# A streaming encoder layer on one core: two more block pairs by Strassen products, sums of activations started a step sooner, and a planner that counts GpSimd

## The chip, the cores and the metric

The kernel runs on one core of a Trainium2 chip. The metric is the time of the device in microseconds (us) for one execution, as the median of three runs. Everything is float32 in the inputs and outputs.

## The reference

One layer with 1024 channels on 640 rows (512 of a prompt, 8 sequences of 16 rows), with a LayerNorm ahead of it. One wide projection of the rows, `w_in` of 1024 x 6656, feeds three branches and three gates:

```python
z = x @ w_in
xa, ya, glu, q, gates = jnp.split(z, COL_SPLITS, axis=-1)
xa_c = causal_depthwise_conv(concat([conv_a_prev, xa]), conv_a_w, conv_a_b)        # width 4
h, h_last = rg_lru(xa_c, h_prev, ...)                 # gates by block matmuls, then a scan over positions
out_a = (h * jax.nn.gelu(ya)) @ proj_a
u = glu[..., :D_CONV] * jax.nn.sigmoid(glu[..., D_CONV:])
v = causal_depthwise_conv(concat([conv_b_prev, u]), conv_b_w, conv_b_b)            # width 31
out_b = jax.nn.silu(layer_norm(v, ln_b_g, ln_b_b)) @ proj_b
out_c = mem_cross_attention(q, k, v) @ proj_c         # 4 heads, 256 memory rows
g = jax.nn.sigmoid(gates + b_gate)
merged = g[:, :, 0] * out_a + g[:, :, 1] * out_b + g[:, :, 2] * out_c
x = layer_norm(ALPHA * x + merged @ w_out)
x = layer_norm(ALPHA * x + swiglu(x))
```

The outputs are the rows and the new states and memory keys and values.

## The kernel before

**Numbers and tiles.** Every matmul operand is split into a high and a low part of the type fp32r (ScalarE copies the high part, VectorE subtracts for the low part), and a product is made of three matmuls: high by high, high by low, low by high. Activations lie with channels on the partitions: `xh` and `xl` are eight blocks of 128 channels by 640 rows. A result block of 128 channels by 640 rows takes 8 channel blocks x 3 x 2 halves of 320 rows = 48 matmuls of 128x320 (a direct step, `z_step`). Weights come in through `wr` and are split to `wh` and `wl`.

**Strassen pairs.** The gate blocks of branch A are made two at a time: `Pair` holds a weight tile of 1024 x 256, and `seven` makes seven products (m1 to m7) of 12 matmuls with sums of weight quarters (`sums_1`, `sums_2`, four VectorE operations of 128x512) and sums of activation quarters. VectorE adds the results (128x320 each); `put` writes a quarter of the two result blocks, with ScalarE applying the function. The activation sums are made once, by `sums_stream`. In the first pair the products come in another order, and `m3` in a bank of its own.

**The order of the work.** The program is a list of steps (`steps`): each has a weight load, a split, matmuls and an evacuation. Between the parts of a step, `advance` lets streams emit instructions: generators for the branch work, in the order of the list `streams`. Each stream goes on while the planned time of VectorE or ScalarE, kept by the `Engine` class from fixed prices, lies behind TensorE's planned time. `yield None` ends a stream's turn until the next call. So the order on each engine is set when the program is written out, and each engine works its own queue in that order. The steps in order: branch A's inputs, query and GLU blocks, gates of branch C, `proj_c`, gates of branch B with `proj_b`, eight GELU blocks (`C_YA`, `ya_evac`), four gate pairs of branch A (`C_G`), `proj_a`, `w_out`, and the feed-forward part, which also uses pairs.

**Around the change.** `ln_b_stream` normalises branch B over its 512 channels, which lie on partitions: GpSimd adds the four channel blocks (`total`, seen at lines 853 and 855 of the profile), a matmul with `ones` sums over the partitions into a bank `pv`, and VectorE subtracts the mean; ScalarE squares, GpSimd adds again, and so on. `lru_stream` runs the convolution of width 4 (taps with `pa` on VectorE), the gates and the scan of branch A; at its end `hout` is transposed on TensorE. `a_stream` multiplies h by the GELU block and splits it (`aT`), one channel block after the other, for `proj_a`. The softmax of the attention (`nm`, exponentials, `rc`) runs beside these. Banks: `pu` is the name of four banks, two for each direct step, that are released when the step's result was evacuated; `pv` is the name of two double banks for side work, counted by `side`, `room` and `over`.

## Time and profile before

| | us |
|---|---|
| Median of three runs (their range) | 1100.15 (1099.13 to 1100.48) |
| The profiled execution's own time | 1099.67 |
| Its span in the trace | 1097.9 |
| TensorE busy | 1061.7 (97%) |
| VectorE busy | 802.9 (73%) |
| ScalarE busy | 490.1 (45%) |
| GpSimd busy | 165.3 (15%) |
| First GELU block's matmuls start | 433.5 |
| First gate pair of branch A | 490.6 |
| `proj_a` starts | 542.77 |

How to read the rows: in the engine shares, busy time, share of the span, and number of instructions. In a window: its start and end, then for PE (TensorE), PEld (weight loads), DVE (VectorE), ACT (ScalarE) and POOL (GpSimd) the busy time and the instructions, the clock that TensorE was granted, the share of busy DMA engines and their GB/s. In a timeline: start, length, engine, line, operation with output and inputs (buffer numbers left out), shapes, how many in a row, and in square brackets the idle time just before and what ended it. In a chain: start, length, engine, output. In a group: line, engine, operation and shapes with a count, busy time and mean ns of one, idle time before and what ended it. Nearly every operation of TensorE, VectorE and ScalarE is recorded at line 64, that of the helper that passes it on, so tiles and shapes tell them apart.

### The profile page before, as it was taken

What the parts mean: (1) busy time and instruction counts of PE and PEld (TensorE: products, weight loads), DVE (VectorE), ACT (ScalarE), POOL (GpSimd) and SP (SyncE); (2) the same over time, 40 slices, a digit from 0 to 9 for tenths busy, and PEclk for the clock granted to TensorE, in tenths of its full rate; (3) what the DMA queues carried; (4) which work ended last, traced back from release to release, by engine and by line L of the source; (5) the groups of instructions that cost most, each with busy time, mean ns of one, the idle gap of its engine ahead of it and who ended that gap; (6) DMA issues with size and microseconds to landing.
All of it is one profiled execution on the core that took longest, in us unless ns stands there. A gap on an engine that the chain in (4) does not pass through costs nothing.

```text
span 1097.9 us, 17000 instructions
## 1 busy us (share of the span) xinstructions
PE 1061.7 (97%) x6827; PEld 1005.9 (92%) x6827; DVE 802.9 (73%) x1335; ACT 490.1 (45%) x863; POOL 165.3 (15%) x185
## 2 busy tenths in 40 slices
PE   8799898998999999999999999899999999999997
PEld 6699898997999999999999889899999999888886
DVE  6929898996364873779855678888887887544775
ACT  4532645446648445846523124433444444334341
POOL 3623323556200000010001120000000000100111
PEclk9999999998999999999999999999999999999999
DMA  9732123352412121212325331132222322734481
GB/s 340 253 95 78 39 67 97 118 154 65 147 52 83 59 96 59 95 45 78 115 78 172 135 134 59 39 101 92 77 78 85 108 77 78 287 115 137 162 289 45
DMA packets 80334, 123.11 MB, mean 112 GB/s; under 512 B 4075, under 2 KB 59371, under 8 KB 80256
## 3 DMA queue, kind: packets, MB, share of 16 engines
q1 hardware_dynamic: 73168, 100.36, 27.6%
q0 software_dynamic: 7088, 21.68, 6.2%
q8 instruction: 53, 0.87, 0.3%
q14 instruction: 25, 0.20, 0.1%
HBM read 112.41 MB, written 9.61 MB: 111 GB/s over the span
## 4 chain that ended last, share of the span: by engine, by line
PE 70%; DVE 11%; ACT 4%; issue 1%; DVEq 0%; ACTq 0%
PE pu L64 62%; DVE s L64 10%; PE pv L64 8%; ACT s L64 3%; ACT L64 1%; DVE wl L64 1%; ACT wh L64 0%; DVE xres L64 0%; DVE mx L64 0%; DVE wh L64 0%; DVE xl L64 0%; DVE nm L64 0%; DVEq L1955 0%; ACT wl L64 0%; DVE st L64 0%
## 5 line engine op out<-in xcount | busy, mean ns | idle before, releaser
L64 PE MATMUL pu<-xh,wh 128*128 128x320 f32 x1040 | 252.6, 315 | 8.3 <-ACT s L64 7.1
L64 PE MATMUL pu<-xh,wl 128*128 128x320 f32 x1040 | 246.9, 310 | 0.0
L64 ACT ACTIVATE wh<-wr 128x1024 fp32r<-128x1024 f32 (+1 forms) x149 | 134.9, 908 | 229.1 <-PE pu L64 123.2
L64 PE MATMUL pu<-xl,wh 128*128 128x320 f32 x888 | 219.7, 311 | 0.0
L64 PEld LDWEIGHTS pu<-xh,wh 128*128 128x128 f32 x1040 | 178.1, 190 | 13.2 <-ACT s L64 9.1
L64 PE MATMUL pu<-s,wh 128*128 128x320 f32 x1064 | 185.5, 310 | 1.9 <-DVE s L64 1.3
L64 PEld LDWEIGHTS pu<-xh,wl 128*128 128x128 f32 x1040 | 177.4, 189 | 0.1
L64 DVE TENSOR_TENSOR s<-s,s 128x640 fp32r<-128x640 f32 (+4 forms) x176 | 124.5, 723 | 65.5 <-ACT s L64 63.3
L64 PEld LDWEIGHTS pu<-s,wh 128*128 128x128 f32 x1064 | 163.4, 188 | 3.4 <-DVE s L64 2.4
L64 DVE TENSOR_TENSOR wl<-wr,wh 128x1024 fp32r<-128x1024 f32 (+1 forms) x100 | 114.1, 1141 | 66.7 <-ACT wh L64 66.7
L64 PEld LDWEIGHTS pu<-xl,wh 128*128 128x128 f32 x888 | 154.2, 189 | 0.6 <-DVE xl L64 0.6
L64 DVE TENSOR_TENSOR s<-s,pu 128x320 f32<-128x320 f32 x188 | 88.4, 484 | 85.8 <-PE pu L64 83.3
L64 PE MATMUL pu<-s,wl 128*128 128x320 f32 x808 | 147.3, 310 | 0.9 <-DVE s L64 0.9
L64 DVE SCALAR_TENSOR_TENSOR s<-s,pb,s 128x511 f32<-128x511 f32 (+14 forms) x240 | 130.1, 613 | 7.8 <-ACT s L64 7.8
L64 ACT ACTIVATE s<-s 128x640 fp32r<-128x640 f32 (+4 forms) x144 | 87.9, 629 | 101.9 <-DVE s L64 101.8
L64 PEld LDWEIGHTS pu<-s,wl 128*128 128x128 f32 x808 | 126.1, 188 | 1.1 <-issue 1.1
L64 PE MATMUL pu<-wh,s 128*128 128x512 f32 (+1 forms) x396 | 116.2, 386 | 0.3 <-ACT wh L64 0.3
L64 PEld LDWEIGHTS pu<-wh,s 128*128 128x128 f32 x396 | 73.1, 189 | 15.1 <-ACT wh L64 1.2
L64 ACT ACTIVATE s<-pu 128x320 f32<-128x320 f32 (+2 forms) x90 | 36.7, 442 | 68.1 <-PE pu L64 68.0
L64 PE MATMUL pu<-wl,s 128*128 128x512 f32 (+1 forms) x198 | 62.9, 389 | 1.6 <-POOL wl L305 0.8
L305 POOL TENSOR_TENSOR wl<-wr,wh 128x1024 fp32r<-128x1024 f32 x13 | 44.4, 3418 | 81.2 <-ACT wh L64 68.4
L64 PE MATMUL pv<-wh,s 128*128 128x512 f32 (+1 forms) x152 | 48.7, 367 | 0.4 <-DVE xres L64 0.4
(139 smaller groups left out, 1249.0 us busy)
## 6 DMA issues: line engine op xcount, KB each, us to landing
wr<-in_w_in SPq DMA_DIRECT2D x26, 1024.0 KB, 5.1
wr<-in_w_ffn_down SPq DMA_DIRECT2D x19, 1024.0 KB, 5.1
wr<-in_w_ffn_gate SPq DMA_DIRECT2D x11, 1024.0 KB, 5.3
wr<-in_w_ffn_up SPq DMA_DIRECT2D x11, 1024.0 KB, 5.3
s<-in_cache_mem_k POOLq DMA_DIRECT2D x16, 256.0 KB, 7.0
s<-in_cache_mem_v POOLq DMA_DIRECT2D x16, 256.0 KB, 7.2
wr<-in_proj_a SPq DMA_DIRECT2D x4, 1024.0 KB
wr<-in_w_out SPq DMA_DIRECT2D x4, 1024.0 KB, 5.7
```

Of the source, the lines that this page charges most:

```text
L64: return f(*a, **k)
L305: self.eng.tensor_tensor(l, x, f32(h), op=OP.subtract)
```

## The change

Four edits. The GELU blocks 4 to 7 are made as two pairs, set ahead of the four gate pairs in the same call; 0 to 3 stay direct. The stream of the activation sums is put into the list one step sooner, and at its front. In the first pair of a call, which is now a GELU pair, the product m2 gets a bank of its own of the kind `pv`, and VectorE adds the copy of m1 to it. GpSimd gets an `Engine` with prices and thus a planned time; `settle(G)` makes a stream give up its turns until TensorE's planned time reaches GpSimd's, in place of one or two turns. A function `settle` with its default is new. As `G` is passed on by the helper now, its operations are recorded at line 64.

```diff
+def price_pool(e, name, a, k):
+    if name == "dma_start":
+        return 600
+    return 150 + 3.2 * elements(a[0])
...
-    G, S = nc.gpsimd, nc.sync
+    G, S = Engine(nc.gpsimd, price_pool), nc.sync
...
     def advance(few=False):
-        for e in (V, A):
+        for e in (V, A, G):
             e.time = max(e.time, state["since"])
...
+    def settle(*engines):
+
+        t = max(e.time for e in engines or (V, A))
+        yield None
+        while P.time < t:
+            yield None
...
         def total(x):
             y = get([128, T])
+            G.time = max(G.time, V.time, A.time)
             G.tensor_tensor(y, x[0], x[1], op=OP.add)
...
         y = total(vb)
         yield 1
-        yield None
+        yield from settle(G)
         yield from room()
...
         y = total(sq)
         free(*sq)
         yield 1
-        yield None
-        yield None
+        yield from settle(G)
         yield from room()
...
         G.tensor_tensor(rs, ve, mhalf[:, :5], op=OP.pow)
         yield 1
+        yield from settle(G)
         yield from room()
...
             elif n == "m2":
-                put(0, 0, p, None, None)
+                if first:
+                    put(0, 0, p, tmp["a"][:, 0], OP.add)
+                    over()
+                else:
+                    put(0, 0, p, None, None)
...
             products = [PRODUCTS[i] for i in (0, 5, 2, 1, 4, 3)] + [("m3", "x", True, "s4", "22")]
+            products[2] = ("m2", "v", True, "12", "21")
...
-                if opens:
+                if u == "v":
+                    until(lambda: side[0] < 2)
+                    acc[u] = pv()[:, 0, :HT]
+                elif opens:
                     acc[u] = pu(1)[0][:, :HT]
...
-    z_load(C_YA, 4)
-    for j in range(KD):
+    z_load(C_YA, 2)
+    for j in range(4):
         z_step(C_YA + 128 * j, ya_evac(j))
     first["pairs"] = len(steps)
-    pair_steps([(Pair(w_load(w_in, C_G + 128 * j, 7)),
+    parts_of_gel = {}
+    pair_steps([(Pair(w_load(w_in, C_YA + 128 * j, 7)),
+                 through(AF.Gelu_apprx_tanh, lambda i, j=j: slot_of(parts_of_gel, j + i),
+                         lambda i, row, j=j: gel.__setitem__(j + i, row))) for j in (4, 6)] +
+               [(Pair(w_load(w_in, C_G + 128 * j, 7)),
                  through(AF.Sigmoid, ...
...
-        if i == first["pairs"] - 6:
-            streams.insert(len(streams) - 1, ("sums0", sums_stream(lambda: state["i"] >= first["pairs"])))
+        if i == first["pairs"] - 7:
+            streams.insert(0, ("sums0", sums_stream(lambda: state["i"] >= first["pairs"])))
```

The order of the instructions changes with it. TensorE at the norm's first total (the matmul with `ones`), before; `pu<-xh,wh` and so on are matmuls of direct steps, `s_162` is GpSimd's sum, and what a row waits for stands in square brackets:

```order
L64 MATMUL pv<-s_162_2714,ones 128x512 [waits PE_49,Pool_49]
L64 MATMUL pv<-s_162_2714,ones 128x128
L64 MATMUL pu<-xh,wh 128x320 x2
L64 MATMUL pu<-xl,wh 128x320 x2
L64 MATMUL pu<-xh,wl 128x320 x2
...
L64 MATMUL pu<-xh,wh 128x320 [waits Activation_49] x2
L64 MATMUL pu<-xl,wh 128x320 x2
```

The same place now:

```order
L64 MATMUL pu<-xh,wh 128x320 [waits Activation_49] x2
L64 MATMUL pu<-xl,wh 128x320 x2
L64 MATMUL pu<-xh,wl 128x320 [waits Pool_49]
...
L64 MATMUL pv<-s_162_2714,ones 128x512 [waits PE_49,Pool_49]
L64 MATMUL pv<-s_162_2714,ones 128x128
L64 MATMUL pu<-xh,wh 128x320 x2
```

The matmul with `ones` stood 24 matmuls ahead of a step whose first matmul waits for ScalarE to release a bank; now it stands 24 behind that matmul, 48 later in all.

ScalarE at the same place, from the second table load behind the softmax's exponentials to its copies of the transposed probabilities (`pv` 128x16x16), now; `s_169` is the Sigmoid of a gate step that empties its banks, `s_183` to `s_185` are squares of the norm:

```order
L64 ACT_TABLE_LOAD
L64 ACTIVATE s_169_2766<-pu,pa 128x320
...
L64 ACTIVATE s_176_2844<-s_91_1712,pa 128x640
L64 ACTIVATE s_178_2864<-s_113_1886,pa 128x640
L64 ACTIVATE s_183_2903<-s_61_870 128x640
L64 ACTIVATE s_184_2907<-s_76_1316 128x640
L64 ACTIVATE s_185_2911<-s_116_1940 128x640
L64 ACTIVATE wh<-wr 128x1024
L64 ACTIVATE s_186_2930<-s_176_2844 128x640
L64 ACTIVATE s_179_2884<-pv 128x16x16
```

The table load and the Sigmoid stand where they stood. The squares stood ahead of the convolution's begin (`s_176`) before and now stand behind it; a copy of a convolution's result (`s_186`) came ahead of the softmax's copies. On VectorE the six taps of that convolution now stand ahead of the subtractions of the mean on which the squares wait.

VectorE at the start of `proj_a`, before; `s_347<-...,pu` adds the products of the last gate pair, `s_263_4533` is h of channel block 7, multiplied by its GELU block, and the row with `s_346` makes its low part:

```order
L64 TENSOR_TENSOR s_263_4533<-s_263_4533,s_303_5194 128x640
L64 TENSOR_TENSOR s_341_5658<-s_340_5657,pu 128x320
L64 TENSOR_TENSOR wl<-wr,wl 128x512
L64 TENSOR_TENSOR s_346_5716<-s_263_4533,s_345_5715 128x640
L64 TENSOR_TENSOR s_347_5739<-s_341_5658,pu 128x320
L64 TENSOR_TENSOR wl<-wr,wh 128x1024
L64 TENSOR_TENSOR s_344_5696<-s_341_5658,pu 128x320
L64 TENSOR_TENSOR wl<-wr,wh 128x1024
L64 TENSOR_TENSOR s_347_5739<-s_340_5657,pu 128x320
```

Now (`s_351<-s_342` is the add of the last product, `s_249` to `s_262` are h of blocks 4 to 7):

```order
L64 TENSOR_TENSOR s_351_5754<-s_342_5645,pu 128x320
L64 TENSOR_TENSOR s_350_5752<-s_226_3542,s_349_5751 128x640
L64 TENSOR_TENSOR s_249_4121<-s_249_4121,s_308_4987 128x640
L64 TENSOR_TENSOR s_353_5790<-s_249_4121,s_352_5789 128x640
L64 TENSOR_TENSOR s_254_4255<-s_254_4255,s_309_5045 128x640
L64 TENSOR_TENSOR s_355_5795<-s_254_4255,s_354_5794 128x640
L64 TENSOR_TENSOR s_259_4342<-s_259_4342,s_316_5125 128x640
L64 TENSOR_TENSOR s_357_5800<-s_259_4342,s_356_5799 128x640
L64 TENSOR_TENSOR s_262_4417<-s_262_4417,s_317_5163 128x640
L64 TENSOR_TENSOR s_359_5805<-s_262_4417,s_358_5804 128x640
```

The multiplications and low parts of blocks 4 to 7, which stood ahead of the last pair's adds, stand behind the last of them. On TensorE the transposes of `hout` move from ahead of the four gate pairs to 28 matmuls before the first of `proj_a`.

## The prediction

> **What bounds the kernel now.** I read the busy shares first, then the two stages that the change rewrites, then the place of the norm of branch B, row by row.
>
> ```profile
> PE 1061.7 (97%) x6827; PEld 1005.9 (92%) x6827; DVE 802.9 (73%) x1335; ACT 490.1 (45%) x863; POOL 165.3 (15%) x185
> ...
> 433.50:490.60 57.10, 57.06 (x389) 56.72 (x390) 43.29 (x62) 36.69 (x59) 3.69 (x8) 1.00 0.24 76
> 490.60:541.00 50.40, 48.92 (x329) 48.04 (x328) 48.47 (x80) 32.89 (x60) 0.43 (x1) 1.00 0.22 69
> ...
> 406.08 10.56 PE pu L64 x72
> ```
>
> TensorE is busy for 97% of the span, so time falls when matmuls go or when a wait of TensorE goes. In the two windows (eight GELU blocks, then four gate pairs; the columns are PE, PEld, DVE, ACT, POOL, granted clock, DMA share, GB/s) TensorE is full at full clock. VectorE has 57.10 - 43.29 = 13.8 us free in the first and 1.9 us in the second: little, if work is to be added there. A matmul of 128x320 in an unbroken run takes 10.56/72 = 0.147 us.
>
> The largest hole that the change touches is at the norm's first total:
>
> ```profile
> 253.17 2.50 PE L64 MATMUL pv<-s,ones 128*128 128x512 f32 x4 [5.00 <-POOL s L855]
> ...
> 252.61 0.54 DVE nm L64
> 253.21 1.28 ACT L64
> 254.50 1.93 ACT s L64 x8
> 256.45 1.28 ACT L64
> 257.75 0.95 ACT L64 ACTIVATE s<-pu,pa 128x320 f32<-128x320 f32 x2
> 258.58 1.70 ACT L64 ACTIVATE s<-s,rc 128x256 f32<-128x256 f32 x4
> ...
> 250.60:254.00 3.40, 0.83 (x1) 0.50 (x2) 3.37 (x5) 0.79 (x1) 2.42 (x3) 0.50 0.00 0
> 254.00:257.40 3.40, 3.40 (x12) 2.69 (x11) 1.20 (x5) 3.37 (x10) 3.40 (x5) 0.50 0.83 235
> 257.40:260.80 3.40, 3.40 (x25) 3.40 (x24) 0.83 (x3) 3.39 (x8) 2.06 (x5) 1.00 0.76 230
> ...
> 267.99 4.06 PE pu L64 x24
> 272.05 1.01 PE pv L64 x32
> ```
>
> TensorE stands from 253.17 - 5.00 = 248.17 to 253.17 for GpSimd's sum. Then the clock is at half: 0.83 us and 3.40 us of busy time at 0.50 are worth half of that, so 2.1 us more. In all 7.1 us. Meanwhile ScalarE does a table load, the exponentials of a softmax and a second table load, and only then the Sigmoid that empties a gate step's banks (257.75).
>
> **The change, part by part.** *Matmuls.* Two blocks cost 96 matmuls directly and 84 as a pair; two pairs save 24: 24 x 0.147 = **-3.5 us**, as long as TensorE sets the pace in that stage.
>
> *VectorE work of the pairs.* Prices:
>
> ```profile
> L64 DVE TENSOR_TENSOR wl<-wr,wh 128x1024 fp32r<-128x1024 f32 x8 | 9.8, 1220 | 8.6 <-ACT wh L64 8.6
> L64 DVE TENSOR_TENSOR s<-s,wr 128x512 f32<-128x512 f32 x8 | 5.5, 688 | 0.1
> L64 DVE TENSOR_TENSOR wh<-s,wh 128x512 fp32r<-128x512 f32 x8 | 5.5, 686 | 0.6 <-ACT wh L64 0.6
> L64 DVE TENSOR_TENSOR s<-s,pu 128x320 f32<-128x320 f32 x21 | 9.9, 482 | 0.6 <-PE pu L64 0.5
> L64 DVE TENSOR_TENSOR s<-s,s 128x640 f32<-128x640 f32 x24 | 19.5, 819 | 2.5 <-ACT s L64 2.3
> L64 ACT ACTIVATE s<-s 128x640 fp32r<-128x640 f32 x14 | 10.1, 736 | 12.0 <-DVE s L64 12.0
> ```
>
> A pair has four sums of weights (0.69), seven low parts (0.69) and five adds of results (0.48): 10.0 us. The direct blocks needed two low parts of 1.22. So +7.5 us a pair, 15 us for both, plus 0.5 for the one add of the own bank. The free time of both stages was 15.7 us and the stage gets 3.5 us shorter. It does not fit: some 3 us must go elsewhere. The order of the instructions shows where: the end of the LRU, which stood at the first row below, 57.8 us ahead of the projection of branch A, moves into the last gate pair, 28 matmuls (4.1 us) ahead of it. Before, the last low part of h*gelu was made inside the last pair (second row), 3.3 us ahead of the projection (third row); now four products h*gelu with their splits come behind the add of the very last product (fourth row).
>
> ```profile
> 484.95 1.04 PE L64 MATMUL pv<-ident,hout 128*36 128x128 f32 x8
> ...
> 538.70 0.82 DVE L64 TENSOR_TENSOR s<-s,s 128x640 fp32r<-128x640 f32 x1
> ...
> 542.77 0.75 PE L64 MATMUL pu<-s,wh 128*128 128x320 f32 x4
> ...
> 542.97 0.49 DVE L64 TENSOR_TENSOR s<-s,pu 128x320 f32<-128x320 f32 x1
> ```
>
> *Start of the projection.* That add ends 0.69 us behind the projection's first matmul (543.46 against 542.77). Then in VectorE's queue: low part of block 3 (0.74 each with the overlap of two in a row), and for blocks 4 to 7 in turn a multiply 0.82, ScalarE's copy 0.74, low part 0.74, with handing over about 2.36 a block, each waiting for the other engine. Block 7's low part is there at 0.69 + 0.74 + 4 x 2.36 = 10.9 us, and four matmuls follow (0.6): 11.5 us where 48 matmuls need 48 x 0.147 = 7.04. So **+4.4 us**, as six waits of 0.5 to 0.95. Below, 0 if the order's last product does not hold the chain up; above, the 5.9 us that it would be if each handing over took 0.3 more and block 3 the same.
>
> The clock may fall there as well, since a window would be some 40% busy:
>
> ```profile
> 35.50:38.90 3.40, 1.31 (x9) 1.03 (x10) 3.40 (x3) 3.14 (x6) 3.32 (x3) 1.00 0.70 185
> 38.90:42.40 3.50, 3.50 (x10) 2.72 (x9) 3.43 (x7) 1.05 (x2) 2.85 (x2) 0.51 0.83 305
> ...
> 185.70:189.10 3.40, 1.77 (x14) 1.54 (x14) 3.40 (x10) 0.98 (x1) 1.84 (x3) 1.00 1.01 332
> 189.10:192.50 3.40, 3.40 (x28) 3.40 (x27) 3.40 (x9) 1.87 (x7) 0.00 (x0) 1.00 1.01 285
> ```
>
> A stretch with 1.31 of 3.40 us busy was followed by one at 0.51, one with 1.77 was not. At 40% (1.36) it is a toss: between 0 and 1.5 us, I take **+0.8**. The Trainium skill (TensorE: Matmul & The Clock Gate, What's actually happening) says that the half rate comes after at least one idle window of 3.4 us. By it, gaps under 1 us cost nothing in clock and the sum would be 0.8 lower; the first of these two pairs of rows speaks against it, since a window with 1.31 us of work was followed by half clock.
>
> *First pair.* Its third product and its fourth waited here:
>
> ```profile
> 495.30 0.41 PE L64 MATMUL pu<-xh,wh 128*128 128x320 f32 x1 [0.51 <-ACT s L64]
> 501.69 0.67 PE L64 MATMUL pu<-s,wl 128*128 128x320 f32 x3 [0.86 <-DVE s L64]
> ```
>
> The own bank takes away the first (ScalarE's copy no longer holds the accumulation), the sums of activations that start a step sooner the second: -1.37. The added add stands in VectorE's queue ahead of the next one, which gives back some 0.3: **-1.1** (bounds -1.37 and 0).
>
> *The norm.* The first total's matmul moves behind 48 more matmuls. Up to 24 of them TensorE runs on: 248.17 + 24 x 0.147 = 251.7. The next step's first matmul then waits, in the order, for ScalarE: for the banks that the Sigmoid above empties, the first of its two halves done at 257.75 + 0.95/2 = 258.2. Nothing on ScalarE moved ahead of it, so the nm, table, exponentials, table of the rows above stand as they were. The wait that the change removes (5.0 for GpSimd) is thus replaced by one of 258.2 - 251.7 = 6.5 us for ScalarE. Two windows at 0.50 follow, up to 260.8; of that 2.6 us are run at half, 1.3 us lost. So 24 matmuls end at 258.2 + 3.5 + 1.3 = 263.0, the total (half of its 2.50 at full clock) at 264.2, 24 more at 267.8, eight transposes of the softmax (about 0.8, by the row with hout above) at 268.6, 24 more at 272.1. There the value matmuls stood at 272.05 before (last row of the second fence): TensorE itself is no sooner. Their input, four copies on ScalarE, is now queued behind more:
>
> ```profile
> 262.39 1.14 ACT L64 ACTIVATE s<-s 128x512 fp32r<-128x512 f32 x2
> 266.62 0.91 ACT L64 ACTIVATE s<-s,pa 128x640 f32<-128x640 f32 x1
> 267.43 0.92 ACT L64 ACTIVATE s<-pu,pa 128x320 f32<-128x320 f32 x2
> 269.06 1.19 ACT L64 ACTIVATE s<-pv 128x256 f32<-128x256 f32 x4
> ...
> 267.56 6.32 DVE L64 SCALAR_TENSOR_TENSOR s<-s,pa,s 128x511 f32<-128x511 f32 x6 [1.62 <-ACT s L64]
> 275.67 2.85 DVE L64 SCALAR_TENSOR_TENSOR s<-s,pa,s 128x511 f32<-128x511 f32 x6
> ```
>
> ScalarE goes on from 258.58 + 1.70 = 260.3: weight copies (0.9 and 1.1) to 262.2, begin of the convolution, Sigmoid, begin of the next (0.8 each, overlapped) to 264.7, and then three squares of the norm ahead of the copies. The squares need VectorE's subtractions, which now stand behind six taps of the convolution. Those took 6.32 us beside GpSimd's adds and 2.85 without; the adds now come later, so 2.85. I get the taps done at 264.7 + 2.85 = 267.6, the squares at 270.7 (three subtractions of 0.82 and the last square, 0.74), a weight copy, a copy of the convolution's result, and the softmax's copies at 272.6 and 273.1: **+0.6 us** against before (bounds +0.1, TensorE's own 272.1, and +1.2 with GpSimd blocking VectorE once). The Trainium skill (SBUF — State Buffer, Who interferes with whom) says that a VectorE instruction with two inputs in SBUF and a GpSimd instruction that reads SBUF contend for a shared read port. The trace agrees (6.32 against 2.85), and by it a collision with GpSimd's low part of a weight, which moves ahead, is what the upper bound holds.
>
> GpSimd's place in the planner costs nothing by itself: its instructions are the same. Elsewhere in the 300 to 430 us I take two waits of the kind of 0.86 as possible either way.
>
> **Sum:** -3.5 - 1.1 + 0.6 + 4.4 + 0.8 = +1.2 us on the profiled execution's 1099.67 (its span is 1097.9): 1100.9. The median of the runs shown is 0.48 above that execution: **1101.4 us**.
>
> **The rivals.** *(A) The wait at the norm goes in full.* Then TensorE gains 7.1 us where I have +0.6: 1101.4 - 7.7 = 1093.7. For it: the wait for GpSimd is the largest there. Against: the first row behind it on TensorE is in the order tied to ScalarE, and ScalarE's rows up to 258.2 are unmoved. It would take that the exponentials start sooner than 254.5, but they hang on VectorE's nm at 252.61.
>
> *(B) The start of the projection is covered.* If VectorE gets ahead of the last product's add (it would have to be idle there already), 4.4 + 0.8 go: 1096.2. For it: VectorE's order was planned with prices, and TensorE's pace might leave it early. Against: the queue is in order, and the add, the last row of that fence, must come first.
>
> *(C) VectorE becomes the bound in the pairs (slower).* It had 1.9 us free in 50.4; all six pairs now carry the load of the LRU's end. If in the five pairs behind the first a product waits for VectorE as the row with 0.86 does, 5 x 0.86 = 4.3 us: 1105.7. It decides as soon as a pair's VectorE work, 10 us and its share of the LRU, exceeds its 84 x 0.147 = 12.3 us of matmuls. For it: the free time of 15.7 us against 15.5 us of new work and a stage 3.5 us shorter. Against: the LRU's last products can be put off, which is what the order does.
>
> *(D) The saved matmuls are not gained*, since the pairs run at VectorE's pace and no new wait shows more than 0.3 us: 1101.4 + 3.5 = 1104.9.
>
> **How the numbers follow.** The forecast has 0.54 with its own range 1098.6 to 1103.8 (the terms' lower ends: 0.3, 0.5, 0.8 and a chain 1.2 shorter; upper: 1.1, 0.6, 0.7); A 0.08, B 0.14, C 0.18, D 0.06. The range goes from B's 1096.0 to 1105.0; outside it are A and most of C. This kernel's measurement can tell about 0.2% (2.2 us) from no change, so faster is below 1098.0 and slower above 1102.3. A and B are faster, with 0.02 of the forecast: 0.24. C and D are slower, and 0.13 of the forecast: 0.37. The rest is 0.39.
>
> **What would show it.** TensorE has 24 matmuls fewer. The 5.0 us for GpSimd is gone, and a wait of 6 to 7 us for ScalarE stands ahead of a gate step's first matmul, before the total, with a granted clock near 0.5 in the next two windows; were there less than 2 us, the norm's part is wrong and A is right. In the first step of the projection stand six waits of 0.5 to 0.95, by turns for ScalarE and VectorE, with the copies of h*gelu just ahead; if they are missing, B. The eight transposes of hout stand some 4 us ahead of it. The waits 0.51 and 0.86 of the first pair are gone; if further pairs show such waits of VectorE, C. And if the stage from the first GELU block to the projection is not some 4 us shorter than 542.77 - 433.50, D.

## The result, and the profile after

The changed kernel takes 1108.41 us (median of four runs, 1107.94 to 1110.04) against 1099.95 us of the kernel before, timed beside it: a ratio of 1.008, 95% interval 1.0066 to 1.0095. It is slower by 8.5 us; 1101.4 was forecast, with a range up to 1105.0. The profiled execution took 1108.38 us with a span of 1106.6.

To see where the time went, I take matmuls with the same place in both programs and compare when they start. The columns below are stretches between such matmuls, by the times of the kernel before: up to the attention's matmul at 187.6; the norm with the softmax beside it, up to 269.2; the middle, up to the first GELU block at 433.5; the GELU and gate blocks, up to the first matmul of `proj_a` at 542.8; the first two steps of `proj_a`, up to 556.9; and the rest, up to the last matmul. A number is how much longer the stretch is than before, in one profiled execution each. The first column holds no changed work and spans -0.5 to +0.8. In the norm column all measured rows but e2, e7 and e11 run the same program up to that point, and still span +0.5 to +1.9; so a difference of up to about 1.4 us between two cells of a column is not read by itself. The traced executions of e1 and e9 took 1.6 and 2.5 us more than the medians of these runs (1105.82 against 1104.22, 1101.61 against 1099.14), so their rows read high. In e7 eight small matmuls cross the border between norm and middle, so only the sum of the two cells is to be read there.

| kernel | start | norm | middle | GELU, gates | proj_a | rest | sum |
|---|---|---|---|---|---|---|---|
| changed | -0.3 | +1.5 | -2.4 | +3.1 | +7.3 | -0.5 | +8.7 |
| forecast | 0 | +0.6 | 0 | -4.6 | +5.2 | 0 | +1.2 |
| e1 sums back | +0.8 | +1.8 | -2.0 | +3.9 | +1.0 | +0.2 | +5.8 |
| e2 pairs alone | +0.6 | 0.0 | 0.0 | +3.7 | +2.8 | -0.4 | +6.6 |
| e3 settled norm alone | -0.3 | +1.5 | -2.0 | +4.2 | 0.0 | +1.2 | +4.7 |
| e4 no pairs | +0.2 | +1.0 | -2.0 | +2.4 | 0.0 | -0.8 | +0.9 |
| e5 low part first | -0.1 | +1.5 | -2.4 | +3.3 | +7.2 | -1.2 | +8.3 |
| e6 no table swaps | +0.5 | +1.7 | -2.3 | -0.3 | +7.4 | -0.7 | +6.3 |
| e7 settled norm, Sigmoid first | -0.5 | +1.8 | -0.1 | 0.0 | 0.0 | -0.2 | +1.1 |
| e8 sums back, low part first | +0.3 | +1.9 | -1.9 | +2.0 | +0.5 | -1.3 | +1.4 |
| e9 sums behind the LRU | +0.5 | +1.9 | -1.9 | +0.7 | 0.0 | +0.5 | +1.6 |
| e10 one pair | +0.4 | +1.6 | -2.0 | -1.4 | 0.0 | -1.0 | -2.3 |
| e11 own bank, low part first | +0.4 | 0.0 | 0.0 | +1.5 | 0.0 | -1.2 | +0.6 |
| e12 behind the LRU, low part first | 0.0 | +1.5 | -1.9 | +1.9 | 0.0 | -0.9 | +0.5 |
| e13 behind the LRU, no table swaps | +0.4 | +0.5 | -1.5 | -0.2 | 0.0 | -0.9 | -1.8 |
| e14 one pair, low part first | -0.3 | +1.4 | -1.9 | -0.9 | 0.0 | -0.5 | -2.2 |

The rows of the changed kernel, by place. First the busy shares of its page:

```profile
PE 1064.3 (96%) x6803; PEld 1008.4 (91%) x6803; DVE 821.5 (74%) x1365; ACT 497.0 (45%) x877; POOL 164.6 (15%) x185
```

TensorE has 24 matmuls fewer and is still 2.6 us longer busy: matmuls run at half clock in more places. VectorE has 18.6 us more work.

At the norm (timeline):

```profile
252.84 1.28 ACT L64 ACT_TABLE_LOAD   x1 [8.88 <-DVE nm L64]
...
256.09 1.28 ACT L64 ACT_TABLE_LOAD   x1
257.38 0.94 ACT L64 ACTIVATE s<-pu,pa 128x320 f32<-128x320 f32 x2
...
257.96 1.05 PE L64 MATMUL pu<-xh,wh 128*128 128x320 f32 x2 [6.62 <-ACT s L64]
```

The 5.00 us for GpSimd is gone, and 6.62 us for ScalarE stand at the gate step ahead: the two halves of the Sigmoid start at 257.38, behind both table loads.

In the first GELU pair (timeline of TensorE, ScalarE and VectorE, then a window whose columns are PE, PEld, DVE, ACT, POOL, clock, DMA share, GB/s):

```profile
458.53 1.28 ACT L64 ACT_TABLE_LOAD   x1
459.83 1.70 ACT L64 ACTIVATE s<-s,lru 128x640 f32<-128x640 f32 x2
...
462.69 1.28 ACT L64 ACT_TABLE_LOAD   x1
463.98 0.77 ACT L64 ACTIVATE s<-pu 128x320 f32<-128x320 f32 x2
464.63 1.36 ACT L64 ACTIVATE xh<-s 128x640 fp32r<-128x640 f32 x2
...
465.40 1.56 DVE L64 TENSOR_TENSOR xl<-s,xh 128x640 fp32r<-128x640 f32 x2 [8.14 <-ACT xh L64]
466.88 0.68 DVE L64 TENSOR_TENSOR wh<-wr,wh 128x512 fp32r<-128x512 f32 x1
...
467.62 1.09 PE L64 MATMUL pv<-xh,wh 128*128 128x320 f32 x4 [1.96 <-DVE wh L64]
...
457.20:465.40 8.20, 8.20 (x58) 8.19 (x56) 0.07 (x1) 8.10 (x13) 0.00 (x0) 1.00 0.00 0
```

The row of TensorE names VectorE, but VectorE had stood still for 8.14 us: in the window it is busy for 0.07 of 8.20 us and ScalarE for 8.10. ScalarE changes its function table between the LRU's exponentials and the GELU blocks (the rows `ACT_TABLE_LOAD`) and reaches the in-place copies `xh` only at 464.63. VectorE's `xl` waits for them, and the low part of the third product's weights stands behind `xl`. The kernel before has six such loads between 435 and 464 as well, beside direct blocks, and TensorE makes no wait above 0.3 us there: what is new is that a pair's copies stand behind them.

In the second GELU pair:

```profile
487.76 1.28 ACT L64 ACT_TABLE_LOAD   x1
489.05 2.62 ACT L64 ACTIVATE s<-s 128x640 f32<-128x640 f32 x4
491.69 1.28 ACT L64 ACT_TABLE_LOAD   x1
...
494.76 0.41 ACT L64 ACTIVATE s<-pu 128x320 f32<-128x320 f32 x1
...
495.23 0.54 PE L64 MATMUL pu<-xh,wh 128*128 128x320 f32 x1 [2.34 <-ACT s L64]
```

The four roots of the LRU's second group, with a load ahead and one behind, take 487.76 to 492.97; the copy that releases m1's bank comes after them. Behind both waits the clock falls to half:

```profile
468.60:470.30 1.70, 1.70 (x8) 1.70 (x7) 1.67 (x4) 0.00 (x0) 0.00 (x0) 0.50 0.00 0
...
495.80:497.50 1.70, 1.70 (x8) 1.70 (x8) 1.67 (x4) 0.41 (x1) 0.00 (x0) 0.50 0.00 0
```

Each fall lasts 3.41 us (468.05 to 471.46, 495.36 to 498.77), with TensorE busy throughout, so it costs half of that, 1.7 us.

Before, the LRU's four roots stood at 457.96, beside direct blocks. VectorE's last scan of the LRU moved from 478.85 to 534.72:

```profile
457.96 2.62 ACT L64 ACTIVATE s<-s 128x640 f32<-128x640 f32 x4
...
478.85 1.49 DVE L64 TENSOR_TENSOR_SCAN s<-s,s 128x640 f32<-128x640 f32 x1
```

(the kernel before), and in the changed one:

```profile
534.72 1.49 DVE L64 TENSOR_TENSOR_SCAN s<-s,s 128x640 f32<-128x640 f32 x1
```

At the start of `proj_a` (changed kernel, timeline and three windows):

```profile
544.66 0.75 PE L64 MATMUL pu<-s,wh 128*128 128x320 f32 x4
...
544.83 1.23 DVE L64 TENSOR_TENSOR wl<-wr,wh 128x1024 fp32r<-128x1024 f32 x1 [0.40 <-ACT wh L64]
545.98 0.48 DVE L64 TENSOR_TENSOR s<-s,pu 128x320 f32<-128x320 f32 x1
546.38 1.55 DVE L64 TENSOR_TENSOR s<-s,s 128x640 fp32r<-128x640 f32 x2
...
548.73 1.56 DVE L64 TENSOR_TENSOR s<-s,s 128x640 fp32r<-128x640 f32 x2 [0.80 <-ACT s L64]
551.14 1.56 DVE L64 TENSOR_TENSOR s<-s,s 128x640 fp32r<-128x640 f32 x2 [0.85 <-ACT s L64]
553.50 1.56 DVE L64 TENSOR_TENSOR s<-s,s 128x640 fp32r<-128x640 f32 x2 [0.80 <-ACT s L64]
555.87 0.82 DVE L64 TENSOR_TENSOR s<-s,s 128x640 fp32r<-128x640 f32 x1 [0.80 <-ACT s L64]
...
551.17 0.56 PE L64 MATMUL pu<-s,wh 128*128 128x320 f32 x2 [0.70 <-ACT s L64]
553.53 1.76 PE L64 MATMUL pu<-s,wh 128*128 128x320 f32 x4 [0.65 <-ACT s L64]
...
549.80:553.20 3.40, 2.08 (x10) 1.29 (x9) 2.05 (x3) 1.20 (x2) 0.00 (x0) 1.00 0.21 66
553.20:556.60 3.40, 3.01 (x8) 2.03 (x8) 2.29 (x3) 1.01 (x2) 0.00 (x0) 0.53 0.00 0
556.60:560.00 3.40, 3.40 (x13) 3.25 (x13) 3.24 (x6) 1.33 (x2) 0.00 (x0) 0.50 0.00 0
```

The add of the last product comes first (1.3 us behind the first matmul at 544.66, held up by a low part of weights that waited for ScalarE), then block after block, one in 2.36 to 2.41 us, each waiting 0.80 to 0.85 for ScalarE's copy. The clock falls to half for two windows, although no single wait of TensorE here is above 0.70 us.

### The profile page after: what moved, and what is told of

Read it like the earlier page. It is cut to its first block, busy times and chain, and to the rows that moved or that the text cites. A ratio compares the mean times of both kernels' runs of the same rounds, so it can differ in the third digit from the quotient of the medians.

```text
span 1106.6 us, 16996 instructions
## 1 busy us (share of the span) xinstructions
PE 1064.3 (96%) x6803; PEld 1008.4 (91%) x6803; DVE 821.5 (74%) x1365; ACT 497.0 (45%) x877; POOL 164.6 (15%) x185
## 4 chain that ended last, share of the span: by engine, by line
PE 67%; DVE 13%; ACT 4%; issue 1%; DMA 0%; POOL 0%; DVEq 0%; ACTq 0%
PE pu L64 59%; DVE s L64 11%; PE pv L64 8%; ACT s L64 3%; ACT L64 1%; DVE wl L64 1%; ACT wh L64 1%; DVE xres L64 0%; DVE wh L64 0%; DVE mx L64 0%; DMA out<-s 0%; ACT wl L64 0%; POOL out L64 0%; DVE nm L64 0%; DVEq L1981 0%
## 5 line engine op out<-in xcount | busy, mean ns | idle before, releaser
L64 PE MATMUL pu<-xh,wh 128*128 128x320 f32 x992 | 241.9, 316 | 12.9 <-ACT s L64 11.2
L64 PE MATMUL pu<-xh,wl 128*128 128x320 f32 x1008 | 240.6, 311 | 0.3 <-ACT s L64 0.3
L64 PE MATMUL pu<-xl,wh 128*128 128x320 f32 x832 | 208.2, 312 | 1.6 <-DVE xl L64 1.6
L64 PE MATMUL pu<-s,wh 128*128 128x320 f32 x1100 | 194.2, 313 | 2.5 <-ACT s L64 1.8
L64 PEld LDWEIGHTS pu<-xh,wh 128*128 128x128 f32 x992 | 170.6, 191 | 17.4 <-ACT s L64 12.0
L64 PEld LDWEIGHTS pu<-s,wh 128*128 128x128 f32 x1100 | 170.3, 190 | 5.6 <-ACT s L64 3.0
L64 PE MATMUL pu<-s,wl 128*128 128x320 f32 x844 | 155.9, 314 | 0.0
L64 PEld LDWEIGHTS pu<-xl,wh 128*128 128x128 f32 x832 | 145.6, 190 | 2.2 <-DVE xl L64 2.2
L64 PEld LDWEIGHTS pu<-s,wl 128*128 128x128 f32 x844 | 134.7, 192 | 0.0
L64 PE MATMUL pu<-xl,wl 128*128 128x320 f32 x168 | 49.9, 308 | 0.0
```

What stands on the lines that cost most here:

```text
L64: return f(*a, **k)
```

## The experiments

The theories at the start: **theory 1**, ScalarE's queue (the sums at the front of the list push the LRU's exponentials and roots among the pairs, where their table loads hold up what VectorE and TensorE wait for); **theory 2**, VectorE's budget (the pairs' own work does not fit, wherever the sums stand).

**e1: the sums back to their old place.**

```diff
-        if i == first["pairs"] - 7:
-            streams.insert(0, ("sums0", ...))
+        if i == first["pairs"] - 6:
+            streams.insert(len(streams) - 1, ("sums0", ...))
```

> The change with one part undone: the stream of activation sums starts six steps ahead of the pairs again and stands second to last in the list, behind the LRU. Theory 1 (ScalarE's queue: sums at the front of the list push the LRU's second group of exponentials and roots some 8 us later, among the GELU and gate pairs, where its table loads hold up the copies that VectorE and TensorE wait for): the waits of 1.96 us (for wh of VectorE) and 2.34 us (for ScalarE) with their half clock, 6.6 us in all, go, the LRU ends sooner and the stall at proj_a (7.4 us against before) shrinks to under 2; 1108.4 falls to 1095 to 1099, perhaps plus one wait of 1 to 3 us for the later sums. Theory 2 (VectorE's budget: the pairs' own 15 us of VectorE work does not fit, wherever the sums stand): the waits move but stay, 1106 to 1110.

Measured: 1104.22 us, ratio to the kernel before 1.0041 (1.0026 to 1.0055). The stall at `proj_a` fell from 7.3 to 1.0 and the wait at the roots is gone, but the first pair's third product waits longer than ever:

```profile
473.80 1.44 PE L64 MATMUL pv<-xh,wh 128*128 128x320 f32 x4 [6.60 <-DVE wh L64]
```

A wait of 1.70 us is new at 527.88. Half of theory 1 stands (the sums at the front make the LRU late, and that makes the stall; this run also starts them a step later, which e9 takes apart), the other half not: the GELU and gate stretch lost as much as before, and the time lies above the 1095 to 1099 that theory 1 gave.

**e2: the two pairs alone**, put into the kernel before.

```diff
-    z_load(C_YA, 4)
-    for j in range(KD):
+    z_load(C_YA, 2)
+    for j in range(4):
...
+    pair_steps([(Pair(w_load(w_in, C_YA + 128 * j, 7)), through(AF.Gelu_apprx_tanh, ...)) for j in (4, 6)] + [...
```

> The kernel before with only the two GELU pairs: no earlier sums, no own bank, GpSimd unplanned. Theory 1: no sums ahead of the LRU, so the two waits for ScalarE's queue are missing; but in the order most of the products h*gelu still stand behind the last product's add, so proj_a's first step stalls by 5 to 7 us; 1099.95 - 3.5 + 6 + at most 2 for the first pair: 1100 to 1105. Theory 2: the waits in the pairs are there as in the change, 1099.95 - 3.5 + 6.6 + 7.4 = 1110.5 or near it.

Measured: 1106.26 us, ratio 1.0055 (1.0038 to 1.0072), between the two. The stretch is 3.7 longer with 24 matmuls (3.5 us) fewer, so the pairs bring 7.2 us of waits and half clock also without the rest of the change (the longest of six waits are 1.98, 1.48 and 1.04); `proj_a` stalls by 2.8 with the sums behind the LRU.

**e3: the settled norm alone.**

```diff
-    G, S = nc.gpsimd, nc.sync
+    G, S = Engine(nc.gpsimd, price_pool), nc.sync
...
-        yield None
+        yield from settle(G)
```

> The kernel before with only GpSimd's planned time and the settled waits of the norm. Prediction's step: the 5.0 us wait for GpSimd becomes one of 6 to 7 us for ScalarE at the gate step, +0.6 (the changed kernel showed +1.4 there). The changed kernel also lost three waits between 357 and 430 us (0.87, 0.46, 0.43): if they go with the norm's new place, 1099.95 + 1.4 - 2.4 = 1099; if they went with the earlier sums, 1101.4.

Measured: 1103.98 us, ratio 1.0035 (1.0022 to 1.0048). The norm's +1.5 and the middle's -2.0 are both this part's, as is the loss of three waits there. Neither expectation held in the whole: the parts behind changed too, and the first gate pair waited 3.93 us instead of 0.51. The rows (timeline) show why:

```profile
492.75 1.56 DVE L64 TENSOR_TENSOR s<-s,s 128x640 fp32r<-128x640 f32 x2 [0.80 <-ACT s L64]
496.97 1.56 DVE L64 TENSOR_TENSOR xl<-s,xh 128x640 fp32r<-128x640 f32 x2 [2.66 <-ACT xh L64]
...
498.46 0.41 PE L64 MATMUL pu<-xh,wh 128*128 128x320 f32 x1 [3.93 <-ACT s L64]
```

The products h*gelu with their to and fro of VectorE and ScalarE now stand right ahead of the in-place split; in the kernel before they were elsewhere. So a planning edit at 250 us cost 4 us at 498: the wait and the half clock behind it.

**e4: the change without the pairs.**

```diff
-    z_load(C_YA, 2)
-    for j in range(4):
+    z_load(C_YA, 4)
+    for j in range(KD):
         z_step(C_YA + 128 * j, ya_evac(j))
```

> The change without the two GELU pairs (eight direct GELU steps), with the earlier sums, the first pair's own bank and the settled norm. Theory 1: the sums at the front still delay the LRU, but the exponentials fall beside direct steps whose copies TensorE needs only once in 7 us: little is lost; first pair's waits 0.51 and 0.86 gone, norm +1.4, middle -2.4: 1097.5 to 1099. Theory 2: the same; if instead the sums' place costs by itself, whatever is made in pairs, waits of 2 us each show in the first pairs and the time is over 1101.

Measured: 1100.42 us, ratio 1.0005 (0.9996 to 1.0014): no difference that can be told, and between the two expectations. Earlier sums and the own bank did not gain the 1.4 us of the first pair; that stretch is 2.4 longer, with four waits of 0.5 to 0.9.

**e5: the low part ahead of the splits.** The sums are drained one product later, so that in VectorE's queue the row `wh<-wr,wh` stands ahead of the two rows `xl<-s,xh` shown above.

```diff
-            if first and i == 0:
+            if first and i == 1:
                 before = sums_there
...
-            streams.insert(0, ("sums0", sums_stream(lambda: state["i"] >= first["pairs"])))
+            streams.insert(0, ("sums0", sums_stream(lambda: state["i"] >= first["pairs"] + 1)))
```

> The changed kernel with the sums drained one product later: in VectorE's queue the low part of the third product's weights (wh) now stands ahead of the two in-place splits xl instead of behind them, and nothing else is reordered there. Theory 1 (the 1.96 us wait is the place behind a split that waits for ScalarE, not VectorE's own work): the low part can be made at about 462.8, the wait of 1.96 us and the half clock behind it (1.7 us) go, some 0.7 may come back at the fourth product; ya to proj_a falls by 2.5 to 3.7 us: 1104.7 to 1106. Theory 2 (VectorE's budget): the work is the same, so the wait reappears at the next product with its full size: 1108 to 1109.

Measured: 1108.86 us, ratio 1.0082 (1.0065 to 1.0099). The wait came back in three pieces at the next products:

```profile
468.72 0.85 PE L64 MATMUL pu<-s,wl 128*128 128x320 f32 x4 [1.06 <-DVE wl L64]
...
471.85 0.85 PE L64 MATMUL pu<-xh,wh 128*128 128x320 f32 x4 [1.11 <-DVE wh L64]
473.34 0.97 PE L64 MATMUL pu<-s,wl 128*128 128x320 f32 x5 [0.64 <-ACT wh L64]
```

The place of one row is not the cause; what is late is the whole row of work behind ScalarE. As theory 2 said of this run, the wait moved on.

**e6: no table swaps.** Tanh, which shares a table with the exponentials, stands for GELU, planned at GELU's price.

```diff
-            each(A.activation, g, p, AF.Gelu_apprx_tanh)
+            for c in range(2):
+                A.time += A.price(A, "activation", (c2(g)[:, c], p[c], AF.Gelu_apprx_tanh), {})
+                A.engine.activation(c2(g)[:, c], p[c], AF.Tanh)
```

(and the same in the pairs' `through`).

> The changed kernel with Tanh in place of GELU in all eight blocks (branch A's gate is then another function), planned at the price of GELU, so that the order stays; 21 table loads instead of 27, since the LRU's exponentials and Tanh share a table. Theory 1 (ScalarE's queue, of which the table loads between the LRU's exponentials and the GELU blocks are the largest avoidable part: six at 1.28 us between 441 and 464): ScalarE reaches the in-place copies of xh some 5 us sooner, the wait of 1.96 with its half clock goes: 1104 to 1105.5. The wait of 2.34 at 495 hangs on the roots and their two loads and stays, or loses one load. Theory 2: no change, 1107 to 1109.

Measured: 1105.85 us, ratio 1.0053 (1.0038 to 1.0068). The GELU and gate stretch fell from +3.1 to -0.3, and only that one. In ScalarE's rows six of seven loads between 441 and 464 are gone:

```profile
443.74 1.28 ACT L64 ACT_TABLE_LOAD   x1
...
461.98 0.77 ACT L1404 ACTIVATE s<-pu 128x320 f32<-128x320 f32 x2 [3.54 <-PE pu L64]
462.63 1.37 ACT L64 ACTIVATE xh<-s 128x640 fp32r<-128x640 f32 x2
```

ScalarE now waits for TensorE (3.54) ahead of the copies `xh`. Here it was ScalarE's table loads: theory 1 for this wait, whose 1.96 us and 1.7 us of half clock are the 3.4 us that the stretch lost. The wait at the roots stayed, with 2.24.

**e7: the Sigmoid ahead of the softmax** in the kernel with the settled norm alone (e3).

```diff
         pr = [get([128, 2, 256]) for _ in range(2)]
+        flush()
         for h in range(NH):
```

> The kernel before with the settled norm (as in the run of that part alone) and one line more: the pending evacuation of the gate step is issued ahead of the softmax's exponentials. The prediction's mechanism at the norm (the bank is held by a Sigmoid that stands behind the exponentials and two table loads): ScalarE was idle for 8.9 us ahead of the first table load, so the Sigmoid is done by 249, the 6.6 us wait and its half clock go, and GpSimd's sum, due at 253.1, is waited for at most 1.5 us: value matmuls some 5 to 7 us sooner than with the settled norm alone; 1103.98 falls to 1097 to 1099. Rival: GpSimd's sum is late by itself and the wait comes back there as 3 us or more: 1101 to 1103.

Measured: 1101.51 us, ratio 1.0012 (1.0003 to 1.0021). The 6.62 us wait is gone, but norm and middle together are not shorter (+1.7, where e3 has -0.5), and the time is the rival's (1101 to 1103), not the 1097 to 1099 that was expected:

```profile
253.61 1.51 PE L64 MATMUL pv<-s,ones 128*128 128x512 f32 x4 [2.39 <-POOL s L64]
267.16 0.83 PE L64 MATMUL pu<-xh,wh 128*128 128x320 f32 x2 [3.61 <-ACT s L64]
...
263.56 1.70 ACT L64 ACTIVATE s<-s,rc 128x256 f32<-128x256 f32 x4
265.28 1.28 ACT L64 ACT_TABLE_LOAD   x1
266.58 0.95 ACT L64 ACTIVATE s<-pu,pa 128x320 f32<-128x320 f32 x2
```

The next step's Sigmoid stands behind the table load instead, and TensorE waits 2.39 and 3.61. The prediction's mechanism is shown (move the Sigmoid and that wait goes), and so is that two other waits, 6.0 us together, take its place. The 2.5 us that this run gains on e3 come from elsewhere: the first gate pair's wait is back at 0.51 (3.93 in e3).

**e8: e1 with the low part first** (the edits of e1 and e5).

> The changed kernel with the sums second to last in the list and six steps ahead (as in the first run), and the low part of the third product's weights ahead of the in-place splits. There the third product waited 6.60 us. Theory 1: that low part is made before the splits, so 4 to 6 us of it go with 1.7 us of half clock, the fourth product waits in its place for its own sums by 1 to 3 us, and proj_a stays nearly without a stall: 1104.2 falls to 1098 to 1101. Theory 2: the backlog of sums is VectorE work that must be done before the fourth product; the wait moves there nearly whole: 1102.5 to 1104.5.

Measured: 1101.51 us, ratio 1.0015 (1.0005 to 1.0024). The 6.60 us wait became one of 5.69 at the fourth product, and the stretch is 2.0 shorter than in e1; the feed-forward part gained 1.5. Theory 2 for the wait itself; the time lies between what the two theories gave.

**e9: the sums behind the LRU**, still seven steps ahead.

```diff
-            streams.insert(0, ("sums0", ...))
+            streams.insert(len(streams) - 1, ("sums0", ...))
```

> The changed kernel with one word changed: the stream of sums still starts seven steps ahead, but second to last in the list, behind the LRU, instead of at its front. It parts the two halves of that edit. If the place in the list is what delays the LRU's roots and the products h*gelu: the 2.34 us wait at the roots goes and proj_a's stall falls from 7.3 us (against before) to about 0.5 to 1, while the first pair still waits, by 2 to 6.6 us (6.60 where the sums also started a step later): 1099 to 1103. If the start seven steps ahead delays the LRU by itself, proj_a keeps its 7 us: 1107 to 1109.

Measured: 1099.14 us, ratio 0.9995 (0.9985 to 1.0004), 9.3 us less than the change. The stall at `proj_a` is gone altogether, as is the wait at the roots. One wait is left in the pairs, and VectorE's backlog makes most of it (timeline, and a window ahead of it):

```profile
467.29 1.56 DVE L64 TENSOR_TENSOR s<-s,s 128x640 fp32r<-128x640 f32 x2 [1.46 <-ACT s L64]
...
470.98 1.44 PE L64 MATMUL pv<-xh,wh 128*128 128x320 f32 x4 [3.32 <-DVE wh L64]
...
455.30:466.00 10.70, 10.70 (x74) 10.57 (x73) 10.33 (x20) 2.64 (x11) 0.00 (x0) 1.00 0.01 2
```

VectorE is busy for 10.33 of 10.70 us ahead of it, ScalarE for 2.64: the reverse of the window of the changed kernel. ScalarE still has one turn in it: behind the scans VectorE waits 1.46 us for a copy (first row), and from 467.00 to 470.30 both are busy, VectorE for 3.01 and ScalarE for 3.30 us.

**e10: one pair.** Blocks 6 and 7 as a pair, six blocks direct; all else as in the change.

```diff
-    z_load(C_YA, 2)
-    for j in range(4):
+    z_load(C_YA, 3)
+    for j in range(6):
...
-                         lambda i, row, j=j: gel.__setitem__(j + i, row))) for j in (4, 6)] +
+                         lambda i, row, j=j: gel.__setitem__(j + i, row))) for j in (6,)] +
```

> The changed kernel with one GELU pair (blocks 6 and 7) and six direct blocks: 12 matmuls more than in the change (+1.8 us) and 7.5 us less work of VectorE. If the amount of VectorE work decides how many products h*gelu are left behind the last add, proj_a's stall falls from 7.3 to under 3 us; if the place of the sums in the list decides it, it stays above 5. The first pair's waits (1.96 and 2.34 with half clock) hang on the place of the LRU's exponentials on ScalarE and stay in kind. 1103 to 1107.

Measured: 1097.38 us, ratio 0.9975 (0.9965 to 0.9985): faster than both kernels, and 5.6 us below the lower end of what was expected, since the first pair's waits did not stay. The stall at `proj_a` is gone with the sums still at the front, and the stretch is 1.4 us shorter than before, near the 1.8 of its 12 saved matmuls. The waits left in it (0.96 and 0.69) are of the size of the two of the kernel before.

**e11: the own bank and the low part first alone**, in the kernel before.

```diff
+            products[2] = ("m2", "v", True, "12", "21")
...
-            if first and i == 0:
+            if first and i == 1:
                 before = sums_there
```

> The kernel before (direct GELU blocks, sums six steps ahead and second to last, norm as it was) with only the first pair's own bank and the low part of the third product's weights ahead of the in-place splits; both also act on the first pair of the feed-forward part. The waits of before are 0.51 and 0.86 there and 4.32 at the feed-forward's first pair (3.77 with the own bank, 3.2 in two pieces with the low part first as well). If those waits are what is left to gain, -0.5 to -1.4 and -1.1 to -1.6: 1097 to 1098.5, faster than both. Rival: the waits move to the fourth product's low part, no change, 1099.5 to 1100.5.

Measured: 1100.23 us, ratio 1.0004 (0.9995 to 1.0013). The feed-forward part gained 1.2 and the first gate pair lost 1.5, each about what one execution differs from another: nothing on the whole, as the rival said.

**e12: e9 with the low part first** (the edits of e9 and e5).

> The sums seven steps ahead but behind the LRU, two GELU pairs, and the low part of the third product's weights ahead of the in-place splits. Without the last edit the third product waited 3.32 us with half clock behind it, and VectorE was busy without a gap ahead of it (scans of the LRU, then the splits). If the wait is VectorE's whole backlog, it moves to the fourth product nearly whole (2.5 to 3.3 us); if the place behind the splits is what counts, at most 1 us is left. The feed-forward's first pair gains 1 to 1.5 us either way (seen in two runs): 1096 to 1098.

Measured: 1099.67 us, ratio 0.9997 (0.9988 to 1.0007). The wait moved to the fourth product, nearly whole, and the time lies above the 1096 to 1098 that were expected:

```profile
472.98 1.44 PE L64 MATMUL pu<-s,wl 128*128 128x320 f32 x4 [3.18 <-DVE wl L64]
```

**e13: e9 without table swaps** (the edits of e9 and e6).

> The same kernel as with the sums behind the LRU, with Tanh in place of GELU in all eight blocks (another function of branch A's gate) at GELU's planned price, order unchanged. In the changed kernel this edit took away the whole wait of 1.96 and its half clock (3.4 us). If the 3.32 us wait here is ScalarE's table loads too, it goes: 1095 to 1096.5. If it is VectorE's backlog of scans, it stays within 0.7 us: 1098 to 1099.5.

Measured: 1098.88 us, ratio 0.9992 (0.9983 to 1.0001). The wait did not change by a hundredth:

```profile
469.93 1.44 PE L64 MATMUL pv<-xh,wh 128*128 128x320 f32 x4 [3.32 <-DVE wh L64]
```

So the same matmul waits for two different reasons: in the change for ScalarE's table loads (e6); with the sums behind the LRU the table loads have no part, and the window of e9 puts it down to VectorE's scans and splits.

**e14: e10 with the low part first.**

> One GELU pair (blocks 6 and 7), sums at the front, and the low part of the third product's weights ahead of the in-place splits. With one pair the order left no product h*gelu behind the last add and proj_a did not stall (1097.4). If the low part's place acts as in the kernel before, the feed-forward's first pair gains 0.7 to 1.0 and the first pair of branch A neither gains nor loses over 0.5: 1096 to 1097.3. If the waits only move, 1097 to 1098.

Measured: 1097.63 us, ratio 0.9983 (0.9974 to 0.9992), the same as e10 within the intervals: with one pair nothing is left in the first pair that this edit moves (waits of 0.96 and 0.63), and the feed-forward part's shorter wait (2.75 for 3.77) does not show in the time.

## Why the prediction was wrong

*The matmuls, right.* 24 fewer, and where no wait stands they cost what was said, 0.147 us each.

*The first pair, wrong in sign, and the step that failed.* The prediction took 1.1 us off ("the own bank takes away the first ..., the sums of activations that start a step sooner the second") and let the pairs' work hide, all but its end. The stretch of GELU and gate blocks, forecast at -3.5 - 1.1 = -4.6, came out at +3.1: 7.7 us too low, which is the whole miss (1108.41 - 1101.4 = 7.0), since the other stretches' errors nearly cancel. The sum had no term for a wait in the pairs; two came, of 1.96 and 2.34 us, with 1.7 us of half clock behind each, 7.7 us together. The two waits of before (0.51 and 0.86) are gone from the first gate pair, and -3.5 - 1.4 + 7.7 makes +2.8 of the +3.1. The working counted VectorE's microseconds over the two stages and never walked ScalarE's queue there. The amount was right: VectorE was short of room, and the order put the rest behind the last add. What it missed is when ScalarE serves it. With the sums at the front of the list, the LRU's second group came later, its exponentials between the last direct blocks and the first pair and its roots into the second; each step there changes tables at 1.28 us, and everything that VectorE had to do was queued behind one copy (0.07 us of work in 8.20). Without the loads the first goes (e6), with the LRU ahead of the sums the second (e9). The rival C (a product of each pair waits 0.86 us for VectorE, 1105.7) had the side and 4.3 of these 7.7 us, and the wrong mechanism: not five short waits of VectorE, but two long ones that ScalarE made. With the sums behind the LRU, the wait of 3.32 us is mostly VectorE's (e9, e13); there C has the engine right, though not the five short waits. The sign that was set for D, a stretch that does not get shorter, did come, but with waits far above the 0.3 us that D allowed, so it does not speak for D.

*The start of `proj_a`, right in mechanism, short in size.* Forecast were +4.4 for the chain and +0.8 for the clock, together 5.2; measured 7.3. The chain ran as written, at 2.36 to 2.41 us a block against 2.36, but it began later: the last product's add ended at 546.46, 1.8 us behind the projection's first matmul and not 0.69, since a low part of weights that waited for ScalarE's copy stands ahead of it. That is 1.1 us. The rest is the clock, from 553.2 to 560.0 at half: with 4.4 + 1.1 the first step would be 5.5 longer, it was 6.3, and the second step 1.0 more; so 1.8 us where 0.8 was taken (bounds 0 to 1.5). In e5 the chain had the full clock until 557.01 and the stall was the same (7.2): of the two windows at half clock, the first cost next to nothing, since the chain set the pace in it. The Trainium skill (TensorE: Matmul & The Clock Gate, What's actually happening) puts the half rate behind at least one idle window of 3.4 us. This trace does not agree: the window from 549.80 to 553.20 had 2.08 us of its 3.40 busy, and half clock followed. The prediction's ground for a fall, a window some 40% busy, holds better than the 2.08 makes it look: 10 matmuls touch that window, and at 0.147 us they are 1.5 us of work, 43%. What decides was not isolated.

*Which cause stands behind that chain.* The prediction named VectorE's lack of room. Two runs show that the full stall takes both: with the sums behind the LRU and two pairs (e9) no stall, with the sums at the front and one pair (e10) none either, with both 7.3. The place of the sums is not the only thing that delays the LRU: the pairs alone, with the sums behind it but six steps ahead (e2), stall by 2.8.

*The norm, right in mechanism.* The wait for GpSimd became one for ScalarE at the gate step, 6.62 us (forecast 6.5); moving the Sigmoid takes it away (e7). The stretch is +1.5 instead of +0.6, slightly above its upper bound (+1.2) and within what one execution differs from another. The Trainium skill (SBUF — State Buffer, Who interferes with whom) says that VectorE's instructions with two inputs in SBUF contend with GpSimd's instructions that read it. The trace agrees: the six taps, now away from GpSimd's adds, took 2.85 us, as in the undisturbed row, and not 6.32.

*The middle, not forecast.* -2.4 us: three waits of the kernel before (0.87, 0.46 and 0.43, from 357 to 430 us) are gone with the settled norm (e3: -2.0). They are 1.8 us, and a wait of 0.69 is new at 432.29; the rest of the -2.4 was not taken apart. The prediction had such shifts in its range and none in its sum. So the settled norm brought about -0.9 with its own place, in the change.

*The rivals A and B* did not happen; A needed the exponentials to start sooner than 254.5, and they did so by no more than 0.4 us.

The own bank and the earlier sums were meant by the prediction to pay 1.1 us in the first pair. No run shows that: without the pairs (e4) and without all else (e11) the stretch grew by 2.4 and 1.5. In the feed-forward part the own bank took 0.6 us off (4.32 to 3.77).

What stays open: what stands behind the six waits of the pairs-only kernel (e2; four of them, 3.9 us, name ScalarE, two, 2.0 us, VectorE), and why the products h*gelu and the splits fall in another order once the norm is settled (e3).

## What to carry to other kernels

Count the work that moves on every engine that serves the busy one, in the order of its queue, and not in sums over a stage: the engine that TensorE named had been idle for 8 us, and the cause was a second engine swapping function tables behind it. When streams share in-order queues, a stream that is put first makes the one behind it late, and its lateness shows further on: here the LRU's last scan came 56 us later, and the last stall stood behind it. Where an engine's slack is nearly used up, half of a gain can be worth more than the whole: here one pair of blocks with the rest of the change brought 2.5 us, two cost 8.5; with the sums behind the LRU two cost nothing and brought nothing (1099.14).

## What the runs showed of the hardware

The granted clock fell to half behind a window of 3.4 us in which TensorE was busy for 2.08 us, with no gap above 0.70 us, and stayed so for a second window; in the kernel before, a stretch with 1.77 of 3.40 busy was not followed by that. Busy time is a poor measure of work there: the matmuls of the first stretch come in groups of two that are recorded as 0.45 to 0.56 us long (551.17 above), where two of an unbroken run take 0.29, so its 10 matmuls are 1.5 us of work, while the second stretch holds 14, 13 of them in one run of 1.82 us. Many short gaps can thus cost through the clock as well (1.8 us here). And swapping a table between two instructions that follow each other cost ScalarE 1.30 to 1.31 us from the end of the one to the start of the next (458.52 to 459.83, the load itself 1.28). The Trainium skill (ScalarE: Activation LUTs, What ACT_TABLE_LOAD costs) adds a drain and comes to 2.66; no such drain shows here. Six such swaps less moved the copies `xh` from 464.63 to 462.63 and the result by 2.6 us (1108.41 to 1105.85).
